# Layer 0's seven-product feed-forward: modulation slices read one step ahead, quarters in two pools, the down part's left operands read a pair ahead

## The chip, the core and the metric

The kernel runs on one core of a Trainium2 chip. The metric is the device time of one execution in microseconds (us); lower is better. The core has a matrix engine (TensorE, PE in the profile), a vector engine (DVE), a scalar engine (ACT), a general engine (POOL, GpSimd) and SP, which here only issues DMAs. Each engine takes its own instructions in the order in which the program has them, and waits at an instruction until the semaphores that it names are set. SP's DMAs therefore form one queue: a DMA that waits for its buffer holds up every DMA behind it.

## The reference

Two layers over 1024 latent and 256 context tokens with 1024 channels; the feed-forward width D_FF is 2816. In each, a mixer and a gated channel mixer (the feed-forward part), both modulated by six vectors per layer which come from a conditioning vector. What matters here:

```python
def _modulation(cond, w, b):
    m = jax.nn.silu(cond) @ w + b
    m = m.reshape(m.shape[:-1] + (6, 1, D_MODEL))
    return jnp.moveaxis(m, -3, 0)

def _conv_ffn(h, w_gate, w_up, conv_w, conv_b, w_down):
    a = h @ w_gate
    ap = jnp.pad(a, ((0, 0), (1, 1), (0, 0)))
    a = ap[:, :-2] * conv_w[0] + ap[:, 1:-1] * conv_w[1] + ap[:, 2:] * conv_w[2] + conv_b
    return (jax.nn.silu(a) * (h @ w_up)) @ w_down
```

The modulation of a layer is a product of 1024 by 6144 for two rows (the latent and the context vector).

## The kernel before

**Seven products.** Layer 0's feed-forward part, `layer0_ffn` (from L880), multiplies 1024 latent tokens by the gate and up weights in blocks of two by two quarters, with seven products instead of eight. Weights and activations are fp32, split into a high and a low part; each product term is three matmuls (L101 to L103 in `mm3`). The quarters of the activations (B11, B21, T1, T2, T3, T4, B22) stay in SBUF as pairs of high and low; T1, B22, T2 and T3 are allocated from one pool `qb`. The quarters F of the transposed stream, from which they are made, are given back after use.

**The loop.** D_FF is worked off in 11 indices p of 256 columns. An index has a gate half and an up half. A half is P1, P2 (12 matmuls 128x512 each), the context tokens' product X (48 matmuls 128x256), then P6, P7, P5, P3, P4 (12 each). The gate products of p = 0 are written out by hand before the loop (`alone`), because the quarters are only made there: P1, P2, P6, P7, P5, P3, P4. At P1 of a half, `weights` loads the raw weights of the next half (two tiles of 512 KB, L75), casts them to their high parts on ACT (L927), makes the low parts (L928, DVE and POOL) and their sums and differences S1 to S4. The gate half's convolution and the elementwise work are on ACT and DVE; the results go to DRAM as `gs`: one quarter (L1119), then two (L1141) and four (L1142) at the end of an index.

**Modulation steps.** Where PE has work for long, the kernel also makes modulation vectors that later stages need. A unit (layer, vector) is eight steps; a step is one 512 KB slice of `ada_w` (L314) and four fp32 matmuls of 32 columns (L316, eight records in a trace). `ada_steps` is a generator: each `next` allocates a slice, loads it, and issues its matmuls. In the loop, `next` stands after P1 of a gate half and of an up half, 20 times for 24 steps of the units (0,5), (1,0), (1,1); the four that are left run behind the loop (`for _ in steps`). The slice comes from the pool `wp` under the tag `raw`, three buffers, which gate and up weights (and, later, the down weights L1370) use as well: a load waits for the reader of the buffer's previous content.

**The down part.** `ffn_down` (L1436) multiplies `gs` by the down weights, again by seven products in the order of `DOWN`: P1, P5, P6, P4, P7, P3, P2, each over five blocks of 128 tokens for layer 0, 33 matmuls of 128x512 a block. P1's left operands are split from tiles that the loop's end loads; those of the others come from `left`: for every second block it reads a pair of blocks from `gs` (`sr<-gs`, 1408 KB, L1471), and for each block casts it to `sh` on ACT (L1475) and subtracts to `sl` on DVE (L1476). The right operands (`down.right`) are made from the down weights, with a sum or difference on DVE first (L1429, L1433, into X0 to X5), and ACT's cast and DVE's difference (L1441, L1442).

**Behind it.** The end of `layer0_ffn` transposes the result per 256 tokens and multiplies it by two weight columns into `hv`; `ada_steps` runs there for the units (1,2) and (1,3), three steps per block, with what is left in the stage behind.

The order of instructions on each engine is set by the tile scheduler from the order in the code, with waits made from the buffers; a part under `tc.high_priority()` goes ahead of what is ready beside it.

Of the kernel before, what the change touches and what calls it, by code (L numbers as in the profile page):

```python
# [11 lines left out]
F32 = mybir.dt.float32  # L12
# [4 lines left out]
ALU = mybir.AluOpType  # L17
# [12 lines left out]
P = 128  # L30
D = 1024
# [3 lines left out]
KD = D // P  # L35
# [24 lines left out]
class Kernel:  # L60
# [243 lines left out]
    def ada_unit(self, ps, tag, l, v, wp, bufs):  # L304

        nc, I = self.nc, self.I
# [12 lines left out]
        nc.vector.tensor_tensor(out=row, in0=acc[:, :256], in1=row, op=ALU.add)  # L319
        if v in (2, 5):  # L320
            for g in range(4):
                nc.sync.dma_start(self.mg[l, v // 3, :, 256 * g:256 * g + 256], row[32 * g:32 * g + 2, :])
            return
# [3 lines left out]
        m = self.mods[l, v]  # L327
        src = pt[:, :256].rearrange("p (j g r) -> p j g r", j=2, g=4)[:, :, :, 0:2].rearrange("p j g r -> p r g j")
        nc.vector.tensor_copy(m.rearrange("p r (g j) -> p r g j", j=2), src)
        if v in (1, 4):  # L330
            for r in range(2):
                nc.vector.scalar_tensor_tensor(
                    out=m[:, r, :], in0=m[:, r, :], scalar=1.0,
                    in1=self.ng[:, l, 0 if v == 1 else 2, :], op0=ALU.add, op1=ALU.mult)

# [543 lines left out]
    def layer0_ffn(self, eh):  # L879
# [10 lines left out]
        with ExitStack() as ec:  # L890
            with ExitStack() as el, ExitStack() as ep:
# [14 lines left out]
                with ExitStack() as e1:  # L906
                    qb = pool(e1, "qb", side="right")
                    for name in ("T1", "B22", "T2", "T3"):
                        Q[name] = self.quarter(qb, name)
# [96 lines left out]
                    part("T2", F["B11"], every)  # L1006
# [48 lines left out]
                    steps = self.ada_steps(ps, "ada", [(0, 5), (1, 0), (1, 1)])  # L1055
                    for p in range(NP):
# [30 lines left out]
                        if p == 0:  # L1087
                            conv_context(x)
                            for n in ("P1", "P6", "P2", "P7", "P5", "P3", "P4"):
                                gather(n, accs[n], g11, g12, g21, g22)  # L1090
                            conv(0)
                            conv(1)
                        else:
                            for n, acc in products(wg, g11, g12, g21, g22):
                                if n == "P1":
                                    wu = weights("ffn_w_up", p)
                                    next(steps, None)
                                elif n == "X":
                                    conv_context(acc)
                                elif n == "P3":  # L1100
                                    conv(0)
                                elif n == "P4":
                                    conv(1)
# [53 lines left out]
            with ExitStack() as eb:  # L1157
# [3 lines left out]
                steps = self.ada_steps(psv, "ada", [(1, 2), (1, 3)])  # L1161
                for b0 in (512, 768, 0, 256, 1024):
                    tt = b0 // P
                    self.to_feature([psx], tb, C[tt:tt + 2], h, b0, 1, 0, 256, 2, None)
                    for _ in range(3):
                        next(steps, None)
# [280 lines left out]
    def ffn_down(self, l, gs, bank, down, accs, ctiles=None, then=None):  # L1447
# [6 lines left out]
        with ExitStack() as es:  # L1454
            right = lambda name, bufs=1: es.enter_context(tc.tile_pool(name=name, bufs=bufs, side="right", reuse_waits="tile"))
            if l:
                sp, cp = right("dS", 2), right("dC")
                tp = es.enter_context(tc.tile_pool(name="dT", bufs=1, reuse_waits="tile"))
            else:
                sp, cp, tp = right("dS", 2), ctiles, None  # L1460
            ex = ExitStack()
# [3 lines left out]

            def left(n, q):
                i = self.DOWN[n][1]
                if q % 2 == 0:
                    n = 256 if q < 4 else P
                    self.sraw = sp.tile([P, NP, 256], F32, tag="sr", name="sr")  # L1470
                    nc.sync.dma_start(self.sraw[:, :, :n], gs[i, :, :, q * P:q * P + n].rearrange("p f t -> f p t"))  # L1471
# [10 lines left out]
            for n, (name, _, b) in enumerate(self.DOWN):  # L1482
# [6 lines left out]
                for q in range(nq):  # L1489
                    if lefts and (n, q) > (0, nq - 2):  # L1490
                        ready.append(left(*lefts.pop(0)))
                    if n < 6 and (l or q < 2):
                        down.right(n + 1, 2 * q, 2 * q + 2)
# [542 lines left out]
```

## Time and profile before

| what | us |
| --- | --- |
| median of 3 runs | 3283.21 |
| the three runs | 3278.65, 3283.21, 3287.43 |
| the profiled execution | 3285.26 |
| its span in the trace | 3283.5 |
| mean granted clock of TensorE, share of full | 0.962 |

The span runs from the first to the last instruction in the trace; the execution's own time is 1.8 us more. In the page, PE, PEld (weight loads into the array), DVE, ACT, POOL and SP are the engines; L316 is line 316 of the kernel before, and `out<-in` names the tiles of an instruction. A row of the list of waits reads "engine output line <- what it waited for: us in total, times, longest". A row of the timeline has start, duration, engine, line, operation, and in square brackets the idle time before it with its releaser. Lines behind the change are moved by 37 to 56.

### The profile page before, as it was taken

Reading aid. Unit: us, or ns where it says so; the run is one execution under the profiler, and the core shown is the slowest. Engines: PE = TensorE matmul, PEld = TensorE weight load, DVE = VectorE, ACT = ScalarE, POOL = GpSimd, SP = SyncE. Lnnn points to the kernel's source line nnn. Section 1 sums busy time; section 2 is a strip of 40 time slices with the busy share of each in tenths; the row PEclk is TensorE's granted clock in tenths of the full one; section 3 lists DMA queues with packets and bytes.
Section 4 is the critical chain, followed back from the end, with each engine's and each line's share of the span. In section 5 each row is a group of like instructions: output and inputs, shape, how many; then the busy total and the mean of one; then the engine's idle time right before and its main releaser. Section 6 shows DMA issues by size and latency. Waiting matters only on the chain. (4 is left out here: it accounts for less than half of the span.)

```text
span 3283.5 us, 41673 instructions
## 1 busy us (share of the span) xinstructions
PE 3023.4 (92%) x16135; PEld 2503.0 (76%) x16135; DVE 1942.6 (59%) x2671; ACT 1262.4 (38%) x2056; POOL 792.9 (24%) x568
## 2 busy tenths in 40 slices
PE   6998999979888898989989998998899999999998
PEld 4986887767777677768778787887698778888787
DVE  4254885566565665656652424445555598778685
ACT  4222786442222222223433233332675443333343
POOL 2122223022121212100211224332321235545001
PEclk7999999989999999999999999999999999999999
DMA  7555333312322322475743442113533323333784
GB/s 232 166 179 175 87 86 121 126 54 73 108 79 80 105 72 88 158 243 180 247 137 130 136 143 66 34 34 98 188 104 124 109 77 103 116 97 97 252 285 152
DMA packets 314379, 422.10 MB, mean 129 GB/s; under 512 B 20497, under 2 KB 226246, under 8 KB 314182
## 3 DMA queue, kind: packets, MB, share of 16 engines
q1 hardware_dynamic: 282102, 376.67, 36.4%
q10 hardware_dynamic: 32080, 42.78, 3.7%
q8 instruction: 127, 2.08, 0.3%
q14 instruction: 70, 0.57, 0.1%
HBM read 312.45 MB, written 106.92 MB: 128 GB/s over the span
## 5 line engine op out<-in xcount | busy, mean ns | idle before, releaser
L101 PE MATMUL acc<-hhi,whi 128*128 128x512 f32 (+3 forms) x632 | 236.1, 374 | 0.0
L928 POOL TENSOR_TENSOR wlo<-raw,whi 128x1024 fp32r<-128x1024 f32 (+1 forms) x44 | 101.8, 2313 | 543.6 <-ACT whi L927 543.6
L103 PE MATMUL acc<-hhi,wlo 128*128 128x512 f32 (+3 forms) x632 | 230.4, 365 | 1.2 <-POOL wlo L92 1.2
L102 PE MATMUL acc<-hlo,whi 128*128 128x512 f32 (+3 forms) x632 | 229.8, 364 | 0.0
L927 ACT CAST whi<-raw 128x512 fp32r<-128x512 f32 x132 | 86.9, 689 | 351.2 <-PE X L102 174.6
L357 POOL TENSOR_TENSOR ss<-ss,mhalf 128x1 f32<-128x1 f32 (+1 forms) x122 | 76.3, 627 | 552.8 <-DVE ss L356 550.2
L92 POOL TENSOR_TENSOR wlo<-raw,whi 128x1024 fp32r<-128x1024 f32 (+1 forms) x41 | 98.4, 2404 | 325.7 <-ACT whi L91 302.1
L316 PE MATMUL ada<-raw,sT 128*32 128x256 f32 x768 | 74.8, 470 | 108.1 <-DMA raw<-in_ada_w 107.7
L101 PE MATMUL acc<-whi,hhi 128*128 128x256 f32 (+1 forms) x464 | 143.4, 313 | 3.9 <-DVE hhi L378 3.9
L928 DVE TENSOR_TENSOR wlo<-raw,whi 128x512 fp32r<-128x512 f32 x88 | 56.9, 687 | 152.1 <-ACT whi L927 152.0
L102 PE MATMUL acc<-wlo,hhi 128*128 128x256 f32 (+1 forms) x464 | 139.8, 306 | 3.2 <-POOL wlo L92 3.2
L194 POOL TENSOR_TENSOR wlo<-raw,whi 128x512 fp32r<-128x512 f32 (+1 forms) x66 | 113.6, 1734 | 113.1 <-ACT whi L193 113.1
L103 PE MATMUL acc<-whi,hlo 128*128 128x256 f32 (+1 forms) x464 | 139.6, 310 | 1.1 <-POOL hlo L380 0.6
L1475 ACT CAST sh<-sr 128x1408 fp32r<-128x1408 f32 x54 | 73.9, 1372 | 170.4 <-PE pp L102 105.0
L103 PEld LDWEIGHTS acc<-hhi,wlo 128*128 128x128 f32 (+1 forms) x632 | 118.3, 187 | 21.1 <-POOL wlo L92 1.7
L101 PEld LDWEIGHTS acc<-hhi,whi 128*128 128x128 f32 (+1 forms) x632 | 118.3, 187 | 21.1 <-issue 2.1
L102 PEld LDWEIGHTS acc<-hlo,whi 128*128 128x128 f32 (+1 forms) x632 | 118.6, 188 | 17.3
L316 PEld LDWEIGHTS ada<-raw,sT 128*32 128x32 f32 x768 | 19.5, 119 | 139.1 <-DMA raw<-in_ada_w 103.0
L194 POOL TENSOR_TENSOR wlo<-st,whi 128x1024 fp32r<-128x1024 f32 x40 | 97.0, 2428 | 99.6 <-ACT whi L193 93.9
L101 PE MATMUL X<-Hch,whi 128*128 128x256 f32 x352 | 111.4, 316 | 0.0
L102 PE MATMUL X<-Hcl,whi 128*128 128x256 f32 x352 | 110.2, 313 | 0.0
L103 PE MATMUL X<-Hch,wlo 128*128 128x256 f32 x352 | 109.1, 310 | 0.0
(837 smaller groups left out, 9517.1 us busy)
## 6 DMA issues: line engine op xcount, KB each, us to landing
raw<-in_ada_w SPq DMA_DIRECT2D x96, 512.0 KB, 4.6
raw<-in_ffn_w_down SPq DMA_DIRECT2D x94, 512.0 KB, 4.8
sr<-gs SPq DMA_DIRECT2D x24, 1408.0 KB, 6.8
raw<-in_ffn_w_gate SPq DMA_DIRECT2D x44, 512.0 KB, 4.6
raw<-in_ffn_w_up SPq DMA_DIRECT2D x44, 512.0 KB, 3.8
gs<-u SPq DMA_DIRECT2D x11, 1280.0 KB, 7.3
xin<-x SPq DMA_DIRECT2D x26, 512.0 KB, 6.9
raw<-in_od_w_in SPq DMA_DIRECT2D x26, 512.0 KB, 4.3
```

The source lines that it names most:

```text
L92: nc.gpsimd.tensor_tensor(out=lo, in0=raw, in1=hi.bitcast(F32), op=ALU.subtract)
L101: nc.tensor.matmul(out, lh, rh, start=first, stop=False)
L102: nc.tensor.matmul(out, lh, rl, start=False, stop=False)
L103: nc.tensor.matmul(out, ll, rh, start=False, stop=last)
L194: eng.tensor_tensor(out=v(t[1]), in0=x, in1=v(t[0]).bitcast(F32), op=ALU.subtract)
L316: nc.tensor.matmul(acc[32 * g:32 * g + 32, :256], self.sT[:, k, :], raw[:, 256 * g:256 * g + 256], start=k == 0, stop=k == KD - 1)
L357: nc.gpsimd.tensor_tensor(out=ss, in0=ss, in1=self.mhalf[:, :ss.shape[1]], op=ALU.pow)
L927: nc.scalar.copy(v(t[0]), x)
L928: eng.tensor_tensor(out=v(t[1]), in0=x, in1=v(t[0]).bitcast(F32), op=ALU.subtract)
L1475: nc.scalar.copy(hi, x)
```

## The change

Five edits.

1. `ada_ahead` takes the place of `ada_steps` in the loop. It keeps a list of slices in flight: the next step's slice is allocated and loaded right behind the present step's matmuls. The first `next`, in the up half of p = 0, only loads. A third call per index stands after P5 of the gate half, for p < 8. That makes 27 calls: the first load, 24 steps, and one more behind each of the two units that end in a transposition. None is left behind the loop.
2. In the `hv` stage `ada_ahead` loads two slices ahead, and four calls per block stand where three did.
3. The pool `qb` becomes `qb0` (T1, B22) and `qb1` (T2, T3).
4. T2 is cast and split in two parts, under `tc.high_priority()`.
5. In `ffn_down` a new `load_left` reads `sr`: the first pair at the third block of the first product, each next pair when the one before it is taken up. For layer 0 `sr` has a pool of its own, `dR`, with two buffers.

```diff
@@ -317,10 +317,14 @@
                                  start=k == 0, stop=k == KD - 1)
             yield
         nc.vector.tensor_tensor(out=row, in0=acc[:, :256], in1=row, op=ALU.add)
+        self.ada_end(ps, tag, l, v, row)
+
+    def ada_end(self, ps, tag, l, v, row):
+        nc = self.nc
         if v in (2, 5):
             for g in range(4):
                 nc.sync.dma_start(self.mg[l, v // 3, :, 256 * g:256 * g + 256], row[32 * g:32 * g + 2, :])
-            return
+            return False
         pt = ps.tile([P, 512], F32, tag=tag, name="adat")
         for j in range(2):
             nc.tensor.transpose(pt[:, j * P:(j + 1) * P], row[:, j * P:(j + 1) * P], self.ident)
@@ -332,6 +336,39 @@
                 nc.vector.scalar_tensor_tensor(
                     out=m[:, r, :], in0=m[:, r, :], scalar=1.0,
                     in1=self.ng[:, l, 0 if v == 1 else 2, :], op0=ALU.add, op1=ALU.mult)
+        return True
+
+    def ada_ahead(self, ps, tag, units, ahead):
+
+        nc, I = self.nc, self.I
+        todo = [(l, v, k) for l, v in units for k in range(KD)]
+        raws = []
+
+        def load():
+            if todo:
+                l, v, k = todo.pop(0)
+                raws.append(self.wp.tile([P, D], F32, tag="raw", name="raw", bufs=3))
+                nc.sync.dma_start(raws[-1], I["ada_w"][l, k * P:(k + 1) * P, v * D:(v + 1) * D])
+        for _ in range(ahead):
+            load()
+        yield
+        for l, v in units:
+            acc = ps.tile([P, 512], F32, tag=tag, name="ada")
+            row = self.cp.tile([P, 256], F32, tag="mrow", name="mrow", bufs=1)
+            for g in range(4):
+                nc.sync.dma_start(row[32 * g:32 * g + 32, :],
+                                  bass.AP(I["ada_b"].tensor, (l * 6 + v) * D + 256 * g, [[0, 32], [1, 256]]))
+            for k in range(KD):
+                raw = raws.pop(0)
+                for g in range(4):
+                    nc.tensor.matmul(acc[32 * g:32 * g + 32, :256], self.sT[:, k, :], raw[:, 256 * g:256 * g + 256],
+                                     start=k == 0, stop=k == KD - 1)
+                load()
+                if k + 1 == KD:
+                    nc.vector.tensor_tensor(out=row, in0=acc[:, :256], in1=row, op=ALU.add)
+                yield
+            if self.ada_end(ps, tag, l, v, row):
+                yield
 
     def ada_steps(self, ps, tag, units, wp=None, bufs=3):
         for l, v in units:
@@ -904,9 +941,10 @@
                 banks = {"pp": 4, "Y": 1, "X": 2, "ada": 1}
                 bank = lambda tag: ps.tile(F32_512, F32, tag=tag, name=tag, bufs=banks[tag])
                 with ExitStack() as e1:
-                    qb = pool(e1, "qb", side="right")
-                    for name in ("T1", "B22", "T2", "T3"):
-                        Q[name] = self.quarter(qb, name)
+                    for i, names in enumerate((("T1", "B22"), ("T2", "T3"))):
+                        qb = pool(e1, f"qb{i}", side="right")
+                        for name in names:
+                            Q[name] = self.quarter(qb, name)
 
                     def part(name, f, k):
                         hi, lo = [t[:, k, :] for t in Q[name]]
@@ -1003,7 +1041,9 @@
 
                     alone("P1", "pp", "A11", "B11")
                     alone("P2", "pp", "A12", "B21")
-                    part("T2", F["B11"], every)
+                    with tc.high_priority():
+                        for k in (0, 2):
+                            part("T2", F["B11"][:, k:k + 2, :], slice(k, k + 2))
                     alone("P6", "pp", "S2", "T2")
                     part("T3", F["B12"], every)
                     alone("P7", "pp", "S3", "T3")
@@ -1052,7 +1092,7 @@
 
                     fw = pool(e1, "fw")
                     gt = None
-                    steps = self.ada_steps(ps, "ada", [(0, 5), (1, 0), (1, 1)])
+                    steps = self.ada_ahead(ps, "ada", [(0, 5), (1, 0), (1, 1)], 1)
                     for p in range(NP):
                         u = fw.tile([P, 4, 640], F32, tag="u", name="u")
                         if gt is None:
@@ -1097,6 +1137,8 @@
                                     next(steps, None)
                                 elif n == "X":
                                     conv_context(acc)
+                                elif n == "P5" and p < 8:
+                                    next(steps, None)
                                 elif n == "P3":
                                     conv(0)
                                 elif n == "P4":
@@ -1158,11 +1200,12 @@
                 tb = pool(eb, "tb")
                 psx = pool(eb, "psx", space=PSUM)
                 psv = pool(eb, "psv", space=PSUM)
-                steps = self.ada_steps(psv, "ada", [(1, 2), (1, 3)])
+                steps = self.ada_ahead(psv, "ada", [(1, 2), (1, 3)], 2)
+                next(steps)
                 for b0 in (512, 768, 0, 256, 1024):
                     tt = b0 // P
                     self.to_feature([psx], tb, C[tt:tt + 2], h, b0, 1, 0, 256, 2, None)
-                    for _ in range(3):
+                    for _ in range(4):
                         next(steps, None)
                     f = tb.tile([P, 2, 512], F32, tag="rw", name="rw", bufs=2)
                     for i in range(2):
@@ -1456,19 +1499,28 @@
             if l:
                 sp, cp = right("dS", 2), right("dC")
                 tp = es.enter_context(tc.tile_pool(name="dT", bufs=1, reuse_waits="tile"))
+                rp = sp
             else:
                 sp, cp, tp = right("dS", 2), ctiles, None
+                rp = es.enter_context(tc.tile_pool(name="dR", bufs=2, reuse_waits="tile"))
             ex = ExitStack()
             xp = ex.enter_context(tc.tile_pool(name="dX", bufs=1, side="right", reuse_waits="tile"))
             down.open(tp, [xp.tile([P, 2 if j < 5 else 1, 512], F32, name=f"X{j}") for j in range(6)])
             C = [cp.tile([P, D], F32, name=f"C{tt}") for tt in range(2 * nq)]
 
+            sraws, pairs = [], [(n, q) for n in range(1, 7) for q in range(0, nq, 2)]
+
+            def load_left():
+                if pairs:
+                    n, q = pairs.pop(0)
+                    i, m = self.DOWN[n][1], 256 if q < 4 else P
+                    sraws.append(rp.tile([P, NP, 256], F32, tag="sr", name="sr"))
+                    nc.sync.dma_start(sraws[-1][:, :, :m], gs[i, :, :, q * P:q * P + m].rearrange("p f t -> f p t"))
+
             def left(n, q):
-                i = self.DOWN[n][1]
                 if q % 2 == 0:
-                    n = 256 if q < 4 else P
-                    self.sraw = sp.tile([P, NP, 256], F32, tag="sr", name="sr")
-                    nc.sync.dma_start(self.sraw[:, :, :n], gs[i, :, :, q * P:q * P + n].rearrange("p f t -> f p t"))
+                    self.sraw = sraws.pop(0)
+                    load_left()
                 hi = sp.tile([P, NP, P], F32R, tag="sh", name="sh")
                 lo = sp.tile([P, NP, P], F32R, tag="sl", name="sl")
                 x = self.sraw[:, :, (q % 2) * P:(q % 2 + 1) * P]
@@ -1489,6 +1541,8 @@
                 for q in range(nq):
                     if lefts and (n, q) > (0, nq - 2):
                         ready.append(left(*lefts.pop(0)))
+                    if (n, q) == (0, 2):
+                        load_left()
                     if n < 6 and (l or q < 2):
                         down.right(n + 1, 2 * q, 2 * q + 2)
                     S = ready.pop(0)
```

The effect on SP's queue over one index of the loop; in order, `gs<-a` and `gs<-u` are the writes of an index, the others loads. Before:

```order
L1141 DMA gs_5595<-a 128x2x640
L1142 DMA gs_5595<-u 128x4x640
L75 DMA raw<-in_ffn_w_gate 128x4x256 x2
L314 DMA raw<-in_ada_w 128x1024
L75 DMA raw<-in_ffn_w_up 128x4x256
L1119 DMA gs_5595<-a 128x640
L75 DMA raw<-in_ffn_w_up 128x4x256
L314 DMA raw<-in_ada_w 128x1024
```

And now:

```order
L1183 DMA gs_5595<-a 128x2x640
L1184 DMA gs_5595<-u 128x4x640
L351 DMA raw<-in_ada_w 128x1024 x2
L75 DMA raw<-in_ffn_w_gate 128x4x256 x2
L351 DMA raw<-in_ada_w 128x1024
L1161 DMA gs_5595<-a 128x640
L75 DMA raw<-in_ffn_w_up 128x4x256 x2
```

Two slices now stand ahead of the gate weights, and a third behind them; before, each slice stood behind the weights of the same half.

On PE, around a step in an up half (pp and Y are the accumulators of P1 and P2, B11 and B21 their quarters). Before:

```order
L101 MATMUL Y<-B11h,whi 128x512
L102 MATMUL Y<-B11l,whi 128x512
L103 MATMUL Y<-B11h,wlo 128x512
L101 MATMUL pp<-B21h,whi 128x512
...
L101 MATMUL pp<-B21h,whi 128x512
L316 MATMUL ada<-raw,sT 32x256 x4
L102 MATMUL pp<-B21l,whi 128x512
```

And now, there and behind P5 of the gate half (T1 is P5's quarter, B22 that of P3):

```order
L103 MATMUL Y<-B11h,wlo 128x512
L364 MATMUL ada<-raw,sT 32x256 x4
L101 MATMUL pp<-B21h,whi 128x512
```

```order
L103 MATMUL pp<-T1h,wlo 128x512
L364 MATMUL ada<-raw,sT 32x256 x4
L101 MATMUL pp<-B22h,whi 128x512
```

The step moves from the end of P2 to the end of P1, and a second place comes up behind P5.

On SP at the start of the down part, from the last write of `gs`. Before:

```order
L1142 DMA gs_5595<-u 128x4x640
L1370 DMA raw<-in_ffn_w_down 128x1024 x5
L310 DMA mrow<-in_ada_b 32x256 x3
L1370 DMA raw<-in_ffn_w_down 128x1024 x5
L310 DMA mrow<-in_ada_b 32x256
L1370 DMA raw<-in_ffn_w_down 128x1024
L1370 DMA raw<-in_ffn_w_down 128x2x512 x5
L1370 DMA raw<-in_ffn_w_down 128x512
L1471 DMA sr<-gs_5595 128x11x256 x2
```

And now:

```order
L1184 DMA gs_5595<-u 128x4x640
L1518 DMA sr<-gs_5595 128x11x256 x2
L1413 DMA raw<-in_ffn_w_down 128x1024 x3
L1518 DMA sr<-gs_5595 128x11x128
L1413 DMA raw<-in_ffn_w_down 128x1024 x5
L1413 DMA raw<-in_ffn_w_down 128x2x512 x5
L1413 DMA raw<-in_ffn_w_down 128x512
```

The two reads of `sr` that the second product needs go from behind seventeen loads of down weights to the head of the queue; the third stands behind three of them.

## The prediction

> **What bounds the kernel now.** I read the page first, then the list of what TensorE (PE) waited for over layer 0's feed-forward stage, then single stalls in the timeline, then stage by stage windows.
>
> The page's span, the engine totals and the granted clock in 40 slices:
>
> ```profile
> span 3283.5 us, 41673 instructions
> PE 3023.4 (92%) x16135; PEld 2503.0 (76%) x16135; DVE 1942.6 (59%) x2671; ACT 1262.4 (38%) x2056; POOL 792.9 (24%) x568
> ...
> PEclk7999999989999999999999999999999999999999
> ```
>
> PE is busy for 3023.4 of 3283.5 us; the second engine, DVE, for 59%. So time is lost in two ways only: while PE stands, and while it runs below full clock. What PE waited for, first from 640 to 1340 us, then from 1340 to 1600 us:
>
> ```profile
> PE ada L316 <- DMA raw<-in_ada_w: 79.3, 20, 4.3
> PE pp L101 <- ACT T2h L913: 6.5, 1, 6.5
> ```
>
> ```profile
> PE X L101 <- ACT sh L1475: 12.3, 1, 12.3
> PE ada L316 <- DMA raw<-in_ada_w: 3.0, 1, 3.0
> ```
>
> Twenty waits of the same kind make 79.3 us, 4.0 each: PE reaches a modulation step and its slice of ada_w is not there. One of them, with POOL's, SP's and PE's rows, and the clock in windows of 2 us (the columns give busy time per engine, then the clock, the DMA share and GB/s):
>
> ```profile
> 789.39 2.28 POOL L928 TENSOR_TENSOR wlo<-raw,whi 128x512 fp32r<-128x512 f32 x1
> ```
>
> ```profile
> 791.69 0.34 SPq L314 DMA_DIRECT2D raw<-in_ada_w  x1
> ```
>
> ```profile
> 795.27 0.64 PE L316 MATMUL ada<-raw,sT 128*32 128x256 f32 x8 [3.65 <-DMA raw<-in_ada_w]
> ...
> 799.84 0.28 PE L102 MATMUL X<-Hcl,whi 128*128 128x256 f32 x1
> 799.96 0.28 PE L103 MATMUL X<-Hch,wlo 128*128 128x256 f32 x1
> ```
>
> ```profile
> 796.00:798.00 2.00, 2.00 (x8) 1.81 (x9) 0.00 (x0) 0.00 (x0) 0.00 (x0) 0.50 0.38 69
> 798.00:800.00 2.00, 2.00 (x14) 2.00 (x13) 0.00 (x0) 0.00 (x0) 0.00 (x0) 0.65 0.57 201
> 800.00:802.00 2.00, 2.00 (x20) 2.00 (x19) 0.48 (x1) 1.13 (x2) 0.00 (x0) 1.00 0.00 1
> ```
>
> The slice's load is issued at 791.69, in the moment when POOL gives a weight slot back (789.39 + 2.28 = 791.67); PE wanted the slice at 795.27 - 3.65 = 791.62. The wait is therefore the whole transfer. Behind it the clock is 0.50, then 0.65, and back at 1.00 four microseconds later, where the 128x256 matmuls start 0.12 us apart. So each stall costs its 4.0 us and about 2.2 us more (4 us at a mean of 0.55 to 0.6 lose 1.6 to 1.8, a longer case below loses 2.9).
>
> **The loop, worked out.** First and last stalled step, a run of matmuls without a stall, and the windows from the first up half (723.9) through the loop's end (1385.3), the down part's first product, the gap behind it and what follows:
>
> ```profile
> 732.29 1.08 PE L316 MATMUL ada<-raw,sT 128*32 128x256 f32 x8 [4.20 <-DMA raw<-in_ada_w]
> ```
>
> ```profile
> 1336.52 1.08 PE L316 MATMUL ada<-raw,sT 128*32 128x256 f32 x8 [4.23 <-DMA raw<-in_ada_w]
> ```
>
> ```profile
> 803.66 0.40 PE L101 MATMUL pp<-T2h,whi 128*128 128x512 f32 x1
> ...
> 819.96 0.39 PE L102 MATMUL pp<-B11l,whi 128*128 128x512 f32 x1
> ```
>
> ```profile
> 723.90:849.30 125.40, 109.12 (x549) 90.25 (x548) 75.09 (x108) 33.48 (x52) 26.09 (x13) 0.92 0.27 88
> ...
> 1225.00:1385.30 160.30, 144.54 (x727) 119.15 (x729) 100.39 (x130) 46.69 (x65) 33.43 (x15) 0.94 0.33 106
> 1385.30:1431.80 46.50, 43.49 (x199) 33.17 (x198) 30.17 (x40) 12.37 (x15) 0.00 (x0) 0.93 0.80 270
> 1431.80:1444.10 12.30, 0.02 (x1) 0.02 (x1) 8.53 (x10) 7.32 (x11) 0.00 (x0) 0.60 0.98 305
> 1444.10:1460.00 15.90, 15.85 (x61) 12.46 (x62) 10.07 (x8) 2.56 (x2) 0.00 (x0) 0.88 0.67 224
> 2700.00:2800.00 100.00, 100.00 (x433) 80.82 (x432) 79.82 (x90) 31.47 (x39) 52.96 (x27) 1.00 0.34 108
> ```
>
> The steps come (1336.52 - 732.29) / 19 = 31.8 us apart, one per half. What a half needs without a stall: between 803.66 and 819.96 stand 70 matmuls of 128x512, 0.233 each; a half has 84 of them (7 products of 12), 19.6 us, and the context's 48 of 128x256 at 0.12, 5.7 us, together 25.3. The last row shows that such a stream can run unbroken: the same products in layer 1, where no step stands, are 100% busy at clock 1.00.
>
> From 723.9 to 1385.3 lie 661.4 us, 21 halves. After the change they hold all 24 steps of these units. A step at full clock is about 0.6 us (an estimate: the 8 records take 1.08 us start to end at half clock). So 21 x 25.3 + 24 x 0.6 = 545.7, **-116 us**. That the loads come in time is read from the new order: each is queued a step earlier. The step behind P5 stands 20 us after the gate half's start, and its load right behind the u write, some 7 us in; the step after P1 of the up half follows 8 us later, its load is free once the P5 step's matmuls are done; the page's median flight decides:
>
> ```profile
> raw<-in_ada_w SPq DMA_DIRECT2D x96, 512.0 KB, 4.6
> ...
> gs<-u SPq DMA_DIRECT2D x11, 1280.0 KB, 7.3
> ```
>
> 8 - 4.6 leaves 3.4 us for the tightest of the three steps of an index, 10 or more for the others. If a load shares the path with the write and takes 7.3, it still fits. Bounds: -119 (a step at 0.45) to -105 (a half at 25.8, from the last stretch: 1336.52 to 1385.3 is 48.8 us for one step, the rest of its half and one whole half).
>
> The **four steps left over** go. They stand at the start of the window 1385.3 to 1431.8: 46.5 us for 165 matmuls of 0.227, 37.5. That is **-9** (3.0 wait, the rest slow clock and the steps themselves); -7 to -10, since only the order of the weight loads beside them changes.
>
> **The left operands, a pair ahead.** PE stands 12.3 us between the first and the second product of the down part. SP, then ACT:
>
> ```profile
> 1420.31 12.33 SPq L1370 DMA_DIRECT2D raw<-in_ffn_w_down  x7
> 1432.70 1.75 SPq L1471 DMA_DIRECT2D sr<-gs  x2
> ```
>
> ```profile
> 1437.17 1.08 ACT L1441 CAST B21l<-X 128x1024 fp32r<-128x1024 f32 x1
> 1442.67 2.63 ACT L1475 CAST sh<-sr 128x1408 fp32r<-128x1408 f32 x2 [4.42 <-DMA sr<-gs]
> ```
>
> The read of sr is issued at 1432.70, when PE is already done, behind seven weight loads; the cast waits for it. In the new order it stands right behind the last u write, some 38 us earlier relative to that product, and the casts stand ahead of the right operand's. Gone: 12.3 and 1.7 of the clock after it (15.9 us at 0.88). Late next is the right operand: its last casts ended at 1437.17 + 1.08, and now come behind loads that have 2.8 MB of sr ahead of them. PE needs the last piece only at the end of the first block's 33 matmuls (7.5 us), so from the row's 1438.3 it could start near 1434 rather than 1431.8. I take 4 us of new wait between nothing and all 12.3, nearest to that row: **-10**, bounds -14 to +1 (the third sr read waits for DVE's sl and stands ahead of weight loads, which can add a microsecond).
>
> **T2 in two parts, quarters in two pools.** What stands ahead of the cast that P6 waited for:
>
> ```profile
> 678.93 0.62 ACT L927 CAST whi<-raw 128x512 fp32r<-128x512 f32 x1
> 684.15 1.06 ACT L344 ACTIVATE xin<-yt 128x1024 f32<-128x1024 f32 x1 [4.60 <-DVE yt L404]
> ...
> 685.20 1.88 ACT L913 CAST T2h<-FB 128x2048 fp32r<-128x2048 f32 x1
> ```
>
> T2h now stands right behind the cast that ends at 679.6, so P6 can begin near 681 and 6.5 us of wait go. But P7 and P5 need T3l and T1l, which DVE makes where it did, behind the sum that waits for the first up weights: most of the 6.5 turns up one or two products later. **-2**, bounds 0 and -8 (the wait and 1.5 of clock).
>
> **The rest.** In the stage ahead of layer 1's attention, five steps now run ahead of the third transposes, and one load stands behind an x write; PE's wait there may move either way:
>
> ```profile
> PE tr L374 <- ACT hf L376: 5.6, 1, 5.6
> ```
>
> I take **+1**, bounds -3 and +3. Layer 1's down part keeps its pools and almost its order: 0, bounds -2 and +2.
>
> **Sum.** -116 - 9 - 10 - 2 + 1 = -136 us. The profiled execution took 3285.3 us (span 3283.5), 2 above the median of the runs, 3283.2, which differ by 9 among themselves. 3285 - 136 = **3149 us**.
>
> A short new wait is cheaper than an old one. The trace has one of 2.40 us, and the clock in the window behind it:
>
> ```profile
> 1609.19 0.50 PE L103 MATMUL Y<-whi,sl 128*128 128x512 f32 x1 [2.40 <-DVE sl L1476]
> ```
>
> ```profile
> 1609.20:1611.20 2.00, 2.00 (x9) 1.65 (x10) 2.00 (x2) 1.17 (x2) 0.00 (x0) 1.00 0.40 86
> ```
>
> [...]
>
> **Rivals.** (1) *Loads still late in part.* One of the three steps of each index comes late, because SP holds its load behind a gs write that waits for DVE's convolution. For it: SP takes its queue in order, and slack for the step in the up half is 3.4 us. Against: the write's own producers end 7 us into a half. Price: 10 steps at 4.0 + 2.2 = 62, so 3211; with waits of 1 us, which leave the clock alone, 3159.
>
> (2) *The sr wait is only exchanged* for the right operand's: 10 us come back, 3159. For it: the window's DMA share is 0.98, so transfers bound that stretch; against it: DVE and ACT idle there.
>
> (3) *Slower: weights become late.* The raw pool's three slots now hold one slice ahead at nearly all times, so gate and up weights go round in two. Their second load is then issued where the slice's load stood, 5.3 us into a half (791.69), lands 4.6 later, and is cast and split by about 14 us; P1 of the next half wants it at 26. Slack is 12 us, and DVE, 18.8 us busy per half (75.09 in four), could eat it. [...]
>
> (4) *The change does not reach the loads*: SP's order still keeps each slice behind weights. Then a stall goes on costing 6.2 us, and the four steps that move into the loop bring four more: 4 x (6.2 + 0.6) - 9 - 10 - 2 + 1 = +7, so 3292, within 0.3%. The order of SP speaks against it: slices stand first.
>
> **How the numbers follow.** Forecast 3149 (3135 to 3165): 0.58. Rival 1: 0.20, between 3155 and 3211. Rival 2: 0.10. Rivals 3 and 4: 0.04 each. Better than 3135: 0.04. The range 3126 to 3190 takes in the bounds (all best: 3285 - 119 - 10 - 14 - 8 - 3 - 2 = 3129; with a run's spread 3126), rival 2 and most of rival 1, and leaves out rivals 3, 4 and the worst of 1. 0.3%, about what a measurement here can tell from no change, is 10 us: faster 0.92, same 0.04, slower 0.04.
>
> **What would show it.** Right: no ada wait over 1 us from 700 to 1340, the clock there 0.99 or more, halves 25.9 us apart, the down part beginning near 1270. PE's wait ahead of the second down product 2 to 5 us, its cause a right operand. P6 waits under 2 us. Wrong: waits "ada" that remain at one of the three places (rival 1), a wait of P1 or P6 for wlo or whi (rival 3), clock under 0.97 without waits (my price per half is then wrong).

## The result, and the profile after

The changed kernel took 3150.76 us (median of four runs, 3148.03 to 3152.66), the kernel before 3280.93 (four runs, 3277.86 to 3287.43): a ratio of 0.960 with a 95% interval of 0.9583 to 0.9618. The forecast was 3149 with a range of 3126 to 3190.

The page of the changed kernel, the lines that answer to those of before:

```profile
span 3148.7 us, 41670 instructions
PE 2979.4 (95%) x16135; PEld 2469.8 (78%) x16135; DVE 1948.4 (62%) x2672; ACT 1262.2 (40%) x2057; POOL 791.4 (25%) x568
...
PEclk8999999999999999999899999999999999999999
```

The span is 134.8 us shorter, but PE's busy time only 44: the rest were gaps. PE's busy time fell although it does the same work, since matmuls at half clock count as longer (in the trace of before, from 1393 to 1395 us at clock 0.50, 0.63 us instead of 0.39 for one of 128x512). What PE waits for now between 640 and 1240 us, the whole list (in its first row `ada` is only the name of the bank in which P5 of p = 0 is summed), and then the windows of the loop, of the first down product and of the second:

```profile
PE ada L101 <- DVE T1l L952: 4.8, 1, 4.8
PE pp L101 <- DVE yt L440: 3.8, 1, 3.8
PE X L1035 <- DVE Hcl L1040: 2.2, 1, 2.2
PE pp L101 <- ACT gt L1071: 1.2, 1, 1.2
PE tr L166 <- DVE xin L443: 1.0, 1, 1.0
PE X L1035 <- ACT X L1036: 0.5, 1, 0.5
```

```profile
714.60:1275.20 560.60, 560.58 (x3028) 463.76 (x3029) 418.40 (x558) 181.61 (x262) 140.42 (x63) 0.99 0.33 113
1275.20:1313.70 38.50, 38.50 (x166) 31.18 (x165) 22.37 (x28) 11.88 (x15) 0.00 (x0) 1.00 0.79 258
1313.70:1353.20 39.50, 38.67 (x167) 30.81 (x166) 32.64 (x32) 16.70 (x18) 0.00 (x0) 1.00 0.79 257
```

None of the twenty waits for ada_w is left in the loop: PE is busy for 560.58 of 560.60 us. The trace, cut at places that both kernels have:

| stretch | before | after | difference | forecast |
| --- | --- | --- | --- | --- |
| start to the stream's transposes | 657.9 | 659.3 | +1.4 | 0 |
| to the first up half (quarters, T2) | 52.9 | 55.3 | +2.3 | -2 |
| to the first down product (loop) | 674.3 | 560.6 | -113.7 | -116 |
| to the second down product | 58.9 | 38.5 | -20.4 | -9 - 10 |
| to the transposes for hv | 234.4 | 234.6 | +0.2 | 0 |
| to the end | 1605.0 | 1600.4 | -4.6 | +1 |

The first row has the same code in both. The changed kernel's own two traces differ there by 3 us (659.3, and 656.3 in e11), all traces of this document by 6 (654.8 in e5 to 660.8 in e2).

### The profile page after: what moved, and what is told of

It is laid out like the page before. It is cut to its first block, busy times and chain, and to the rows that moved or that the text cites. A ratio compares the mean times of both kernels' runs of the same rounds, so it can differ in the third digit from the quotient of the medians.

```text
span 3148.7 us, 41670 instructions
## 1 busy us (share of the span) xinstructions
PE 2979.4 (95%) x16135; PEld 2469.8 (78%) x16135; DVE 1948.4 (62%) x2672; ACT 1262.2 (40%) x2057; POOL 791.4 (25%) x568
## 5 line engine op out<-in xcount | busy, mean ns | idle before, releaser
L720 PE MATMUL s<-kst,q 128*128 128x512 f32 (+1 forms) x416 | 103.1, 378 | 6.5 <-ACT p L728 6.5
L1528 DVE TENSOR_TENSOR sl<-sr,sh 128x1408 fp32r<-128x1408 f32 x54 | 92.2, 1709 | 22.4 <-ACT sh L1527 22.4
L724 DVE TENSOR_REDUCE nm<-s 128x1 f32<-128x1280 f32 (+1 forms) x80 | 101.1, 1266 | 7.3 <-PE s L720 7.0
L431 POOL TENSOR_TENSOR gb<-gb,ngb 128x1024 f32<-128x1024 f32 x6 | 15.4, 2559 | 343.7 <-DMA gb<-mg 332.6
L103 PE MATMUL X<-Hch,wlo 128*128 128x256 f32 x352 | 99.6, 283 | 0.0
L102 PE MATMUL X<-Hcl,whi 128*128 128x256 f32 x352 | 99.6, 283 | 0.0
```

Source lines behind the costliest of these rows:

```text
L102: nc.tensor.matmul(out, lh, rl, start=False, stop=False)
L103: nc.tensor.matmul(out, ll, rh, start=False, stop=last)
L720: nc.tensor.matmul(t[:, b0:b0 + bn], q[:, e, i, cs], heads[self.d][0][:, e, b0:b0 + bn], start=i == 0, stop=i == 1)
L724: nc.vector.reduce_max(out=self.nm[:, e:e + 1], in_=self.s[e][:, self.w], axis=AX.X, negate=True)
L1528: nc.vector.tensor_tensor(out=lo, in0=x, in1=hi.bitcast(F32), op=ALU.subtract)
```

## The experiments

Each of e1 to e10 is one execution, and the kernel before alone spreads over 9 us (3277.14 to 3286.59 in nine runs). Effects of a few us are therefore read from single stretches of the traces, not from the totals.

**Four parts undone, one at a time** (e1 to e4; the kernel before took 3280.58 beside them). The first loads each slice in its own step and keeps the three places:

```diff
-                    steps = self.ada_ahead(ps, "ada", [(0, 5), (1, 0), (1, 1)], 1)
+                    steps = self.ada_steps(ps, "ada", [(0, 5), (1, 0), (1, 1)])
```

> The changed kernel, but each modulation slice in the loop is loaded in the step that uses it, as before; the three places of the steps per index stay. My theory (the gain of the loop comes from the earlier load, the places alone give nothing): 24 waits for ada_w of about 4 us each from the first up half to the end of the loop, clock there 0.92 to 0.94, the loop from its first up half to the down part 560.6 + 24 x 6.2 = 709 us, the execution near 3150 + 149 = 3299 us. Rival (the new places lie better, or the freed pool slots let the loads start sooner, so part of the gain comes without loading ahead): fewer than 15 waits over 2 us, the loop below 650 us, the execution below 3240 us.

Measured: 3257.05 us. PE's waits in the loop (714 to 1377), the loop's window, and SP around a step behind P5, which PE runs at 784.50:

```profile
PE ada L316 <- DMA raw<-in_ada_w: 67.6, 17, 4.4
```

```profile
714.50:1376.90 662.40, 594.41 (x3028) 489.18 (x3028) 411.71 (x556) 180.62 (x263) 140.35 (x63) 0.93 0.29 95
```

```profile
764.19 0.37 SPq L1184 DMA_DIRECT2D gs<-u  x1
767.84 0.34 SPq L314 DMA_DIRECT2D raw<-in_ada_w  x1
```

Neither expectation held in its count. 17 steps wait, those behind P1; the seven behind P5 don't, since a buffer is free there and SP has nothing ahead of the load, which goes out 17 us early by itself. Per wait the price is near the predicted 6.2: 662.4 - 560.6 = 101.8 us for 17 is 6.0 each (4.0 of wait, 2.0 of clock). So the earlier load brings 102 of the loop's gain; the new place behind P5 would bring its steps without a stall even without it.

The second puts the read of the left operands back to where its block is due, into the pool of sh and sl:

```diff
                 if q % 2 == 0:
-                    self.sraw = sraws.pop(0)
-                    load_left()
+                    i, m = self.DOWN[n][1], 256 if q < 4 else P
+                    self.sraw = sp.tile([P, NP, 256], F32, tag="sr", name="sr")
+                    nc.sync.dma_start(self.sraw[:, :, :m], gs[i, :, :, q * P:q * P + m].rearrange("p f t -> f p t"))
```

> The changed kernel, but the left operands of the down part are read when their block is due and lie in the shared pool again. My theory (that read was late in SP's queue behind the down weights, whatever the loop does): PE waits 10 to 13 us ahead of the second down product for sh, the down part of layer 0 from its first to the end of its second product 90 to 92 us instead of 77.9, the execution near 3163 us. Rival (the four leftover steps and their loads had delayed the queue, so the wait is mostly gone without the read ahead): the wait is under 5 us and the execution below 3156 us.

Measured: 3153.91 us. PE's waits from 1270 to 1340:

```profile
PE X L103 <- DVE sl L1518: 0.9, 1, 0.9
PE X L101 <- ACT sh L1517: 0.6, 1, 0.6
PE pp L103 <- DVE T1l L1446: 0.5, 1, 0.5
```

My theory fell: without the read ahead the wait for sh is 0.6 us, not 12. From the first down product to its second is 39.5 us against 38.5. What did remove the 12.3 us was open.

The third has T2 in one piece without priority, the two pools stay:

```diff
-                    with tc.high_priority():
-                        for k in (0, 2):
-                            part("T2", F["B11"][:, k:k + 2, :], slice(k, k + 2))
+                    part("T2", F["B11"], every)
```

> The changed kernel, but T2 is cast and split in one piece and without priority; the two pools stay. My theory (the priority puts two DVE subtractions for T2 ahead of the read of y, which holds the accumulator that P6 needs, and delays T1's low part behind them): P6 starts 2 to 4 us earlier, no wait of over 2 us for T1's low part, the stretch from the transposes of the stream (659.3 in the changed kernel's trace) to the first up half 49 to 52 us instead of 55.3, the execution 3 to 6 us less, near 3146 us. Rival (the two pools, not the priority, brought the new order, and it costs the same): the stretch stays at 55 us or more.

Measured: 3146.71 us; the stretch is 50.2 us, as expected. Why the priority costs is seen on DVE in the changed kernel, then PE's waits in this one from 656 to 716.

```profile
679.88 3.72 DVE L952 TENSOR_TENSOR T2l<-FB,T2h 128x1024 fp32r<-128x1024 f32 x2 [1.39 <-ACT T2h L951]
...
684.39 1.28 DVE L440 SCALAR_TENSOR_TENSOR yt<-y,ss,gb 128x1024 f32<-128x1024 f32 x1 [0.73 <-POOL ss L394]
685.63 1.76 DVE L975 TENSOR_TENSOR s<-raw 128x512 f32<-128x512 f32 x1
```

```profile
PE pp L102 <- DVE T2l L952: 4.5, 1, 4.5
...
PE pp L101 <- DVE yt L440: 1.3, 1, 1.3
```

P6 waits for DVE's read of y (L440). With the priority, T2's two subtractions run ahead of that read, and P6 starts behind its end, 685.67; without, the wait for it is 1.3 us. P6 then waits 4.5 us for T2's low part, but the 4.8 us for T1's are gone.

The fourth loads the slices of the hv stage in their own step, three per block:

```diff
-                steps = self.ada_ahead(psv, "ada", [(1, 2), (1, 3)], 2)
-                next(steps)
+                steps = self.ada_steps(psv, "ada", [(1, 2), (1, 3)])
...
-                    for _ in range(4):
+                    for _ in range(3):
```

> The changed kernel, but in the stage of hv the slices are loaded in their own step and three steps stand per block, as before. My theory (there the load ahead does not help: the loads stand behind the writes of x in SP's queue, and five steps now stand ahead of transposes that are ready): no wait of 7.7 us for ada_w, the stretch from the end of the down part to the third low-part wait in the stage behind it 103 to 104 us instead of 106.1, the execution 1 to 4 us less, near 3148 us. Rival (the clock, not the order, makes the difference of 2.6 us between the two traces): 106 us as in the changed kernel.

Measured: 3153.07 us. The theory fell: the wait did not go, and the stretch that it named took 105.7 us, as the rival had it. PE's waits in the first 50 us of the stage, in the changed kernel and in this one:

```profile
PE ada L364 <- DMA raw<-in_ada_w: 11.1, 3, 7.7
PE tr L411 <- ACT hf L413: 0.9, 1, 0.9
```

```profile
PE ada L316 <- DMA raw<-in_ada_w: 11.4, 3, 7.8
PE tr L411 <- ACT hf L413: 0.8, 1, 0.8
```

The load ahead does not set these waits. They come with the fifth edit: in each of the ten traces with the read of the left operands ahead, PE's longest wait here is 7.6 to 8.0 us for ada_w; in the four without it (before, e2, e5, e9) it is 5.6 us for hf. By which way is not shown. Over the whole rest of the program the load ahead goes with a shorter time: from the stage's first transposes to the end, the traces without it (before, e4, e5, e9) take 1605.0 to 1609.6 us, the ten with it 1600.4 to 1604.3. The means differ by 4 us; the changed kernel's two traces differ by 2 (1600.4 and 1602.3), and through which waits the load ahead would act is not shown.

**Parts alone, and slack** (e5 to e8; before 3281.41). The loop's edit alone, all else as before:

```diff
-                    steps = self.ada_steps(ps, "ada", [(0, 5), (1, 0), (1, 1)])
+                    steps = self.ada_ahead(ps, "ada", [(0, 5), (1, 0), (1, 1)], 1)
...
+                                elif n == "P5" and p < 8:
+                                    next(steps, None)
```

> The kernel before with the loop's part of the change alone (slices a step ahead, third place behind P5); quarters in one pool, T2 in one piece, left operands read when due, the hv stage as before. Theory after the run without the read ahead (what held the left operands up in SP's queue were the bias rows and slices of the four leftover steps, which the loop's part removes): PE waits less than 2 us for sh ahead of the second down product, the loop takes 560 to 562 us, the execution is near 3281 - 114 - 20 = 3147 us, as fast as the whole change. Rival (my step of the prediction: the read is late behind the down weights themselves): a wait of 10 to 13 us and 3157 us or more.

Measured: 3161.64 us, the loop 559.8. The new theory fell, and the rival held: the wait is back without the leftover steps. PE's wait, and SP:

```profile
PE X L101 <- ACT sh L1513: 9.9, 1, 9.9
```

```profile
1281.50 23.42 SPq L1409 DMA_DIRECT2D raw<-in_ffn_w_down  x14
1304.97 2.56 SPq L1509 DMA_DIRECT2D sr<-gs  x2
```

The converse, the old loop with all other parts kept:

```diff
-                    steps = self.ada_ahead(ps, "ada", [(0, 5), (1, 0), (1, 1)], 1)
+                    steps = self.ada_steps(ps, "ada", [(0, 5), (1, 0), (1, 1)])
...
-                                elif n == "P5" and p < 8:
-                                    next(steps, None)
```

> The changed kernel with the loop as before (slices loaded in their own step, two places per index, four steps left over); all other parts stay. Both theories expect the loop at 673 to 676 us with 20 waits for ada_w. Theory A (either cure suffices: with the read ahead the left operands are early although the leftover steps are there): no wait for sh over 2 us ahead of the second down product, at most 4 us for its right operand, the execution near 3281 - 10 + 2 = 3273 us. Rival B (the leftover steps delay the down weights too, so the wait changes to the right operand): over 6 us of wait there, 3278 us or more.

Measured: 3275.05 us, with 20 waits for ada_w (80.1 us) in the loop, and for the second down product no wait for sh, and 1.0 us for its right operand: theory A. From the first down product to the second is 42.8 us, 4.3 more than in the changed kernel, and that is what the four leftover steps cost beside the other edits (four steps of about 0.6 us and a wait of 2.1, behind which the clock stayed at 1.00). Without the other edits they cost more: from before to e5 the first product, the wait for sh taken off, went from 58.9 - 12.3 = 46.6 to 48.8 - 9.9 = 38.9 us, 7.7 less. There the steps' wait was 3.0 us, and the clock 0.51 in the six behind it.

Every raw weight of the loop read three times, in a row, into its tile:

```diff
         else:
-            self.nc.sync.dma_start(raw, src)
+            for _ in range(getattr(self, "times", 1)):
+                self.nc.sync.dma_start(raw, src)
```

(`times` is 3 from the loop's start to its end.)

> The changed kernel, with each raw gate and up weight of the loop read three times into its tile, one read after the other, so that weights come at least 9 us later than in the changed kernel (two more flights of 4.6 us), 14 us where both tiles of a half queue up. The prediction's rival 3 put the slack of the weights at 12 us and the point where the change loses its gain at 16. If so: waits of 0 to 3 us per half, for whi or wlo, 20 of them, the execution between 3155 and 3230 us. If the slack is much smaller: over 4 us per half and 3270 us or more; if much larger: no waits and under 3155 us.

Measured: 3196.38 us, inside the band, but not by the expected wait. In the loop, from 715 to 1317:

```profile
PE ada L365 <- DMA raw<-in_ada_w: 13.9, 5, 3.6
PE pp L102 <- DVE u L1075: 5.7, 3, 4.0
PE Y L102 <- DVE gt L1075: 5.0, 1, 5.0
PE ada L365 <- DVE mod L334: 2.9, 1, 2.9
...
PE Y L102 <- ACT whi L966: 0.5, 1, 0.5
```

For weights PE waits 0.5 us in all, so nothing speaks for a slack smaller than the 12 us of the prediction. The 16 us of the expectation is an estimate that no run shows: the forecast's 136 us over 21 halves are 6.5 us each, and less the 2.2 that the prediction took for the clock behind a stall they leave 4.3 us of wait, on top of the slack of 12. In one half that was followed, the low parts that P1 needs were done 4.4 us ahead of it (888.85 for 893.27), in the changed kernel 14.5 (895.21 for 909.75). The loop grows by 41.3 us, through slices that queue up in SP behind the repeated reads and through DVE, which is handed its work later.

T2 in two parts without priority:

```diff
-                    with tc.high_priority():
-                        for k in (0, 2):
-                            part("T2", F["B11"][:, k:k + 2, :], slice(k, k + 2))
+                    for k in (0, 2):
+                        part("T2", F["B11"][:, k:k + 2, :], slice(k, k + 2))
```

> The changed kernel, T2 still cast and split in two parts, but without priority, so that the read of y by DVE stands ahead of them. Theory (the priority does the harm, the halves help, since the first half of the low part is there a microsecond earlier): P6 starts near 681 and waits 3.5 to 4 us for T2's low part instead of 4.5 with one piece; the stretch from the stream's transposes to the first up half 48 to 51 us, the execution near 3145 us. Rival (T1's low part, which now stands behind a sum of up weights on DVE, takes the gain back): a wait of over 2 us for T1's low part and a stretch of 52 us or more.

Measured: 3152.43 us, the stretch 52.1 us: the rival. PE's waits from 656 to 716:

```profile
PE pp L102 <- DVE T2l L952: 2.8, 1, 2.8
PE ada L101 <- DVE T1l L952: 2.2, 1, 2.2
```

T2's wait is 1.7 us shorter than in one piece, and T1's low part, 2.2 us late behind the sum of up weights, takes more than that back.

**What brings the left operands forward, the slices' slack, and the best version** (e9 to e12; before 3279.28, nine runs). The loop's edit with the two pools:

```diff
+                    for i, names in enumerate((("T1", "B22"), ("T2", "T3"))):
+                        qb = pool(e1, f"qb{i}", side="right")
+                        for name in names:
+                            Q[name] = self.quarter(qb, name)
```

(in place of the one pool `qb`, added to e5)

> The loop's part of the change and the two pools of quarters, nothing else (T2 in one piece, left operands read when due, hv stage as before). With the loop's part alone PE waited 9.9 us for sh ahead of the second down product; without only the read ahead it waited 0.6 us. Theory (the two pools bring the read forward, because sr's memory no longer waits for the quarters that the first product still reads): PE waits less than 2 us for sh there and the execution is 10 to 14 us below the loop's part alone, near 3148 us. Rival (the hv stage or T2's priority shifted the order, or the read ahead is needed after all): a wait of 8 us or more and 3157 us or more.

Measured: 3154.70 us. PE's waits around the second down product (from 1265 to 1330), then SP:

```profile
PE pp L103 <- DVE T1l L1443: 0.5, 1, 0.5
PE X L103 <- DVE sl L1515: 0.5, 1, 0.5
```

```profile
1283.76 13.49 SPq L1410 DMA_DIRECT2D raw<-in_ffn_w_down  x9
1297.30 0.46 SPq L1510 DMA_DIRECT2D sr<-gs  x1
```

The theory holds in its place: no wait for sh is left, and the part up to the second product takes 38.7 us instead of 48.8. With the two pools the read stands behind nine down weights, not fourteen, and goes out 11 us ahead of its product (1308.5); in e5 it went out 1.4 us before PE was ready for it (1306.4). The total, 7 us under e5 and not 10 to 14, is short of the expectation by the start (659.1 against 654.8 before the first common place) and the end.

Each slice of the loop read twice into its tile:

```diff
-                nc.sync.dma_start(raws[-1], I["ada_w"][l, k * P:(k + 1) * P, v * D:(v + 1) * D])
+                for _ in range(2 if ahead == 1 else 1):
+                    nc.sync.dma_start(raws[-1], I["ada_w"][l, k * P:(k + 1) * P, v * D:(v + 1) * D])
```

> The changed kernel, with each modulation slice of the loop read twice into its tile, so that it comes one flight of 4.6 us later. The prediction gave the step behind P1 of the up half 3.4 us of slack and the others 10 or more; in the changed kernel's trace that slice is issued at 772.5 and used at 781.0. If so: waits of 0.5 to 2 us at that step alone, at most 10 of them, no loss of clock, the execution 3153 to 3170 us. If the slack is 5 us or more: no waits, under 3155 us. If waits pile up in SP's queue: over 3180 us.

Measured: 3154.09 us, no wait for ada_w in the loop. From 727 to 1270:

```profile
727.00:1270.00 543.00, 543.00 (x2944) 448.62 (x2943) 406.87 (x542) 175.95 (x257) 138.40 (x63) 1.00 0.42 137
```

A second flight fits into the tightest step too: in one index, the reads go out at 876.89 and 880.50, 3.6 us apart, and PE uses the slice at 885.30 without a wait. So its slack was larger than the 3.4 us of the prediction.

Last, the changed kernel again and e3's kernel, five rounds each on the same chip:

> The changed kernel as it is, for comparison with the next one on the same chip: 3151 us, within 3 us.

> The changed kernel with T2 in one piece and without priority, the variant that came out 4 us lower in one look and whose stretch was 5 us shorter in the trace. Theory: 3146 us, 3 to 6 us below the changed kernel on the same chip, its interval apart from the changed kernel's. Rival (the look fell on a good execution): within 2 us of the changed kernel.

Measured: 3151.39 us (3147.86 to 3154.17, five runs; ratio 0.9607, 0.9594 to 0.962) and 3147.33 us (3145.35 to 3147.96, four runs; ratio 0.9594, 0.9581 to 0.9607). 4.1 us apart in the median, but the intervals overlap, so the expectation of intervals apart failed. What is sure is the stretch: 55.7 us in e11's trace, 50.2 in e12's, as in the two traces before (55.3 and 50.2). With T2 in one piece the kernel is the lower of the two by this measure.

## Why the prediction was right

**The loop, -116 forecast, -113.7 measured.** Its steps held: the load in the moment of use was the cause (e1: 17 such loads, 17 stalls), a stall costs its wait and some 2 us of clock (6.0 together in e1), and a half without stalls takes about what its matmuls take. The window that the prediction summed, from P2 of the first up half, took 546.4 us against its 545.7; 1.3 of the 2.3 us that are missing fall in the 14 us ahead of it. Rival 1 (loads late in part) and rival 3 (weights late) did not occur; e10 and e7 show that both had room.

**Leftover steps and left operands, -9 and -10 forecast, -20.4 measured together.** The sum was near, a step of the reason was wrong. The leftover steps took 7.7 of it in the order of before (e5), so 12.7 are left for the left operands. The prediction let the 12.3 us go because the read of sr moves to the head of SP's queue, and gave the two pools no part in it. The runs show another: with the loop's edit alone the wait is 9.9 us; with the two pools added it is gone (e9); and without the read ahead, but with the pools, it is 0.6 us (e2). The pools carry this term, some 10 us (48.8 to 38.7 from e5 to e9), the loop's edit 2.4 of it (12.3 to 9.9), and the read ahead on top of them 0.2 to 1 (38.5 against 38.7 in e9 and 39.5 in e2). Whether the read ahead alone would do the same with one pool was not run. That the pools act through the memory in which sr lies is argued from the order only; that the read goes out behind nine loads instead of fourteen is shown. The right operand, named as late next with 4 us, costs 0.8 in the second product (0.62 and 0.21). The leftover steps, at -9, are worth 7.7 without the other edits and 4.3 beside them (e6), so the terms don't add up one by one.

**T2, -2 forecast, +2.3 measured.** The step that failed: "P6 can begin near 681 and 6.5 us of wait go". P6 needs its accumulator too, and that is held by y until DVE has read it. In the trace of before, the wait was put down to T2h, which came last; DVE had read y from 680.55 to 681.83, so a start near 681 was right only while DVE kept its order. With the priority T2's subtractions went ahead of that read, it came last itself, and P6 began at 685.8. What the prediction did see, that T1's low part would be late next, came on top: 4.8 us of wait and half clock behind it (0.54 from 700 to 704). By e3 and e12 the edit costs 5 us of that stretch, of which the priority makes 3.2 (e8: 52.1 without it) and the two halves 1.9; without the edit the stretch is 2.7 shorter than before, near the -2, and it is the two pools that bring this (e9: 50.6; e5, with one pool: 52.9).

**The hv stage, +1 forecast, -4.6 to the end.** PE's wait there is of another kind (11.1 us for ada_w where it was 8.8 for hf and hhi), with either way of loading (e4); it came with the read of the left operands ahead, for which the prediction had no term here. The program from there on is 4 us shorter in the traces with the load ahead. The term was small, as forecast, and had the wrong sign.

So four terms off by 1 to 6 us cancel in part: +4.3 at T2, -5.6 at the end, -1.4 at the down part, +2.3 in the loop. The start of the sum helped too: it was the profiled execution, 3285.26 us, 4 above the median of before; the medians differ by 130.2 us, not by 136. That the forecast missed by 2 us only is in part luck; that the loop carries most of the gain is not.

## What to carry to other kernels

A DMA that is waited for nearly as long as its own flight (here 4.0 us, with a median flight of 4.6) was issued at the moment of use; look in its queue for what it stood behind, and count the slow matmuls after the gap with the gap (2.0 us on 4.0 in e1). When several edits touch one wait, the sum of a forecast can come out right with the credit in the wrong place: undo them one by one before keeping one. Before a part is given priority, list every releaser of the instruction that waits for it, the accumulator's last reader included (here DVE's read of y, a wait of 3.8 us), and see what the priority pushes back.

## What the runs showed of the hardware that was not expected

A wait of about 2 us can slow the clock or leave it as it is. Here are two waits at a modulation step, each with the window behind it; PE was busy at full clock ahead of both. The first is in e7, the second in e6:

```profile
943.60 1.08 PE L365 MATMUL ada<-raw,sT 128*32 128x256 f32 x8 [2.11 <-DMA raw<-in_ada_w]
```

```profile
943.60:947.60 4.00, 4.00 (x16) 2.64 (x17) 1.88 (x4) 1.92 (x4) 0.00 (x0) 0.57 0.92 291
```

```profile
1394.61 0.64 PE L316 MATMUL ada<-raw,sT 128*32 128x256 f32 x8 [2.09 <-DMA raw<-in_ada_w]
```

```profile
1394.60:1398.60 4.00, 3.99 (x23) 2.90 (x23) 3.09 (x5) 0.00 (x0) 0.00 (x0) 1.00 1.09 364
```

The clock is 0.57 behind 2.11 us and 1.00 behind 2.09. In e8, P6's first matmul came after 1.37 us of waiting, the next after 2.81 more:

```profile
684.00 0.47 PE L101 MATMUL pp<-T2h,whi 128*128 128x512 f32 x1 [1.37 <-DVE yt L440]
687.28 0.50 PE L102 MATMUL pp<-T2l,whi 128*128 128x512 f32 x1 [2.81 <-DVE T2l L952]
```

```profile
687.30:691.30 4.00, 4.00 (x11) 3.14 (x12) 3.94 (x4) 0.07 (x2) 0.53 (x1) 0.57 0.56 212
```

The clock is 0.57 there too. Whether the two gaps add up is not shown, since the longer one may do it alone, as the 2.11 us in e7 did. The prediction's remark that a short wait is cheap rests on one wait of 2.40 us that left the clock at 1.00. In the same trace the 2.98 us ahead of a leftover step were followed by 0.51 (1390.8 to 1396.8 us), the 3.65 us ahead of a step in the loop by 0.50 (796 to 798), and in e7 2.11 us, less than those 2.40, by 0.57: in these runs the length of a wait alone does not tell. What decides near 2 us is not shown by them.

Repeated reads cost the loop nothing by their traffic alone: in e10 DMA moved 137 GB/s from 727 to 1270 us, where the changed kernel moved 114, with PE busy throughout at clock 1.00.
